# Another order of the first MLP product's seven parts

## The chip, the cores and the metric

The kernel runs on one core of a Trainium2 chip. The metric is the time of one execution on the device in microseconds. The kernel before took 2326.77 us (median of three runs, 2323.07 to 2330.35).

## What is computed

One decoder layer over 2048 tokens of width 1024, all in float32: a norm, an input projection, four token mixers, a group norm, an output projection with a residual, and then the part that matters here, a squared-ReLU MLP of inner width 4096 with a residual and a final norm.

```
h = rms_norm(x, norm2_g)                         # 2048 x 1024
x = x + square(relu(h @ w_mlp_in)) @ w_mlp_out   # 1024x4096, 4096x1024
return rms_norm(x, final_g)
```

## The kernel before, in words

Every float32 product is made of three matmuls in a rounded format. `split` (lines 53 to 58) writes the high part of an operand with a cast on ScalarE (line 54) and the remainder with a subtraction on VectorE (line 58); a product is then high times high, high times low and low times high.

The MLP (class `MLP`) works on halves of 1024 tokens, the second half of the sequence first. Within a half the inner width is cut into two chunks (`c`), and for each chunk there is a first product (tokens times `w_mlp_in`, called IN here) and a second one (hidden times `w_mlp_out`, OUT). So the MLP has eight stages: IN, OUT, IN, OUT for one half and the same for the other. Each stage is a product of two matrices of 2 x 2 blocks, and it is done with seven block products in place of eight, in the manner of Strassen. The tables `FIRST` (for IN) and `SECOND` (for OUT) give for each of the seven the weight blocks, the token or hidden blocks and the blocks of the result: an entry `((a), (b), sign)` is block a plus or minus block b, and with `None` for b it is block a alone. In `FIRST` a token block (k, t) is the half k of the model width and the 512 tokens t of the half; a weight block is (half of the chunk's inner width, half of the model width).

A product has 8 steps (`p`), and a step of an IN stage is 12 matmuls into one PSUM bank of the pool `ps_i`, which has three. What a step needs and leaves:

- the weight side, made two steps ahead (`AHEAD`): one or two loads of 256 KB on SP's queue (lines 1492 and 1508); for a pair of blocks POOL adds or subtracts them (`united`, line 1485); then the cast and the subtraction of `split`;
- the token side, made once for a product, while the product before runs (`tokens_side`, called from `run` at steps 1 to 5): four times one or two loads of `hT` (line 1492), for a pair an addition on POOL (line 1485), and the split into `bh` and `bl`. There are two buffers of each;
- the result: `product_in` takes the PSUM bank to one or two of the four hidden blocks `c`. The first product in the order that reaches a block copies it with ScalarE (line 1563), later ones add to it with VectorE (`gather`, lines 1573 and 1575), and after the last one ScalarE does relu and square in place (lines 1568 and 1569).

`run` works out from the order which product is the first and the last for each block (`ends`). By the place in the order, not by the product, it loads the residual rows `acc` (fourth place, chunk 0) and gets the norm and the transposes of the other half out of `prep` (places one to seven of the first half's second IN stage). OUT stages have their own order, `OUT_ORDER`. Their hidden side (`hidden_side`, line 1544) adds two hidden blocks on POOL for five of the seven products; its result is the tile `s`. `weight_sums` writes sums of `w_mlp_out` blocks to memory during the first half's OUT stages, so that the later stages load them as one block.

Ahead of the MLP stand the mixers and the output projection. While the last rows of the projection run, `prep` normalises the first half's tokens in groups of 256 and stores their transpose `hT` (lines 1460 to 1479) in memory: sixteen tiles, by 512 tokens and 256 columns of the width.

Inside the MLP the order of instructions on each engine is not written out. The program lists the steps, and a planner that simulates the engines gives each instruction a place: an instruction whose operands are there by the simulation can go ahead of earlier ones that still wait. On the chip each engine then runs its list strictly in this order, and waits on semaphores.

Of the kernel before, what the change touches and what calls it, by code (L numbers as in the profile page):

```python
# [1393 lines left out]
}  # L1394
IN_ORDER = (1, 4, 5, 7, 3, 2, 6)
OUT_ORDER = (3, 5, 6, 1, 2, 4, 7)
AHEAD = 2

# [25 lines left out]
class MLP:  # L1424
# [172 lines left out]
    def run(self):  # L1597
# [9 lines left out]
        ends = {}  # L1607
        for order, table, n in ((IN_ORDER, FIRST, 0), (OUT_ORDER, SECOND, 1)):
            seen, last = {}, {}
            for i in order:  # L1610
                for blk, _ in table[i][2]:
# [3 lines left out]
        steps = [(half, c, out, i, p) for half in self.halves for c in range(self.NC) for out in range(2)  # L1615
                 for i in (OUT_ORDER if out else IN_ORDER) for p in range(NP)]
        made, sides = {}, {}
# [25 lines left out]
        for n, (half, c, out, i, p) in enumerate(steps):  # L1643
            if c == 0 and not out and i == IN_ORDER[3]:
                self.acc[p] = accp.tile([128, self.D], F32, tag=f"acc{p}", name="acc")
                with behind(self.tc, SP):
                    nc.sync.dma_start(out=self.acc[p], in_=self.x1[half * self.HT // 128 + p])
            if c == 1 and not out:

                if i == IN_ORDER[0] and p == 0:  # L1650
                    k = self.halves.index(half) + 1
                    more = self.prep(self.halves[k]) if k < len(self.halves) else iter(())
                if n % 4:
                    next(more, None)
                if i == IN_ORDER[-1]:
                    for _ in more:
# [187 lines left out]
```

## Time and profile before

| what | value |
|---|---|
| median of the runs | 2326.77 us |
| the profiled execution: time, span | 2332.89 us, 2331.2 us |
| PE busy | 2156.8 us (93%) |
| VectorE (DVE) busy | 1775.0 us (76%) |
| ScalarE (ACT) busy | 1166.4 us (50%) |
| GpSimd (POOL) busy | 952.8 us (41%) |
| mean granted clock of PE, share of full speed | 0.971 |
| the MLP: first matmul to last | 989.34 to 2312.81 us |

The profile is of one execution. Times in the rows are microseconds from the start of the span, unless ns is said. PE is the matmul engine, PEld its weight loads, SP the engine that issues most loads. A wait is named by the instruction that released it, as `<-ACT bh L54`. L1485 is line 1485 of the kernel. A row of the table by windows gives the window, its length, the busy time of PE, PEld, DVE, ACT and POOL with their instructions (x), PE's mean granted clock as a share of full speed, the busy share of the DMA engines and GB/s.

### The profile page before, as it was taken

The numbers are of one execution on the slowest core, as the hardware profiler recorded it, in microseconds if no ns is written. First come the engines' busy times: TensorE is split into PE (matmuls) and PEld (weight loads), VectorE is DVE, ScalarE is ACT, GpSimd is POOL, SyncE is SP. The second block draws the span as 40 slices with busy tenths as digits, with TensorE's granted clock in tenths as the row PEclk, the third lists the DMA queues.
The fourth block names the chain that finished last, engine by engine and source line by source line (L and its number), as shares of the span: only waits on it lengthen the run. The fifth ranks groups of instructions, "written<-read, shape, count | busy, mean of one in ns | idle before, by whom it ended". The sixth has DMA issues, their size and how long they took to land.

```text
span 2331.2 us, 32435 instructions
## 1 busy us (share of the span) xinstructions
PE 2156.8 (93%) x10077; PEld 1758.3 (75%) x10077; DVE 1775.0 (76%) x3826; ACT 1166.4 (50%) x2349; POOL 952.8 (41%) x988
## 2 busy tenths in 40 slices
PE   5999998997999998799998999898989999999996
PEld 4777777776887887578777777787878787888885
DVE  5887757765676775378899868888878798578797
ACT  4423544444666664257633356543557643567443
POOL 2144343231001011154877633657244665246352
PEclk9999999998999999999999999999999999999998
DMA  7533135237666746999989688979699634578223
GB/s 183 164 83 95 62 96 169 89 131 226 194 173 167 196 139 203 246 260 320 279 239 224 206 252 255 268 211 221 183 281 289 212 114 122 164 224 243 96 82 113
DMA packets 398236, 435.53 MB, mean 187 GB/s; under 512 B 37552, under 2 KB 280272, under 8 KB 397808
## 3 DMA queue, kind: packets, MB, share of 16 engines
q1 hardware_dynamic: 370224, 362.08, 52.1%
q0 software_dynamic: 23232, 65.09, 11.5%
q10 hardware_dynamic: 4608, 6.29, 0.7%
q8 instruction: 80, 1.31, 0.2%
q14 instruction: 92, 0.75, 0.1%
HBM read 370.35 MB, written 96.57 MB: 200 GB/s over the span
## 4 chain that ended last, share of the span: by engine, by line
PE 48%; DVE 9%; DMA 9%; issue 6%; POOL 4%; ACT 3%; SPq 1%; POOLq 0%; DVEq 0%; ACTq 0%
PE po L1583 6%; PE po L1584 6%; PE po L1582 6%; PE pi L1557 5%; PE pi L1559 5%; PE pi L1558 5%; POOL raw L1485 3%; DMA raw<-in_w_mlp_in_dram 3%; DVE wl L58 2%; PE s L1080 2%; PE t L50 2%; PE po L1356 2%; PE po L1358 2%; PE po L1357 2%; DMA raw<-hT 1%
## 5 line engine op out<-in xcount | busy, mean ns | idle before, releaser
L1485 POOL TENSOR_TENSOR raw<-raw 128x512 f32<-128x512 f32 x304 | 447.4, 1485 | 359.8 <-DMA raw<-in_w_mlp_in_dram 188.5
L58 DVE TENSOR_TENSOR wl<-raw,wh 128x512 fp32r<-128x512 f32 x448 | 423.7, 952 | 63.4 <-ACT wh L54 54.6
L1557 PE MATMUL pi<-bh,wh 128*128 128x512 f32 x896 | 357.5, 399 | 36.5 <-ACT c L1563 12.0
L1583 PE MATMUL po<-wl,sh 128*128 128x512 f32 x896 | 352.8, 394 | 22.2 <-DVE wl L58 22.2
L1558 PE MATMUL pi<-bl,wh 128*128 128x512 f32 x896 | 353.6, 395 | 5.8 <-DVE bl L58 5.8
L1559 PE MATMUL pi<-bh,wl 128*128 128x512 f32 x896 | 353.8, 395 | 5.1 <-DVE wl L58 5.1
L1582 PE MATMUL po<-wh,sh 128*128 128x512 f32 x896 | 351.3, 392 | 2.1 <-ACT wh L54 2.1
L1584 PE MATMUL po<-wh,sl 128*128 128x512 f32 x896 | 351.9, 393 | 0.0
L1544 POOL TENSOR_TENSOR s<-c 128x512 f32<-128x512 f32 x160 | 256.1, 1611 | 234.3 <-DVE sl L58 201.8
L54 ACT CAST wh<-raw 128x512 fp32r<-128x512 f32 x448 | 274.5, 615 | 120.0 <-POOL raw L1485 51.4
L58 DVE TENSOR_TENSOR sl<-s,sh 128x512 fp32r<-128x512 f32 x160 | 207.9, 1307 | 35.4 <-ACT sh L54 35.1
L1557 PEld LDWEIGHTS pi<-bh,wh 128*128 128x128 f32 x896 | 170.8, 191 | 80.8 <-ACT c L1563 15.8
L54 ACT CAST sh<-s 128x512 fp32r<-128x512 f32 x160 | 99.4, 621 | 258.7 <-PE po L1583 184.5
L1583 PEld LDWEIGHTS po<-wl,sh 128*128 128x128 f32 x896 | 170.0, 190 | 61.8 <-DVE wl L58 26.3
L1559 PEld LDWEIGHTS pi<-bh,wl 128*128 128x128 f32 x896 | 171.0, 191 | 44.4 <-DVE wl L58 8.1
L1558 PEld LDWEIGHTS pi<-bl,wh 128*128 128x128 f32 x896 | 170.9, 191 | 41.2 <-DVE bl L58 6.3
L1582 PEld LDWEIGHTS po<-wh,sh 128*128 128x128 f32 x896 | 170.0, 190 | 38.0 <-ACT wh L54 2.5
L1584 PEld LDWEIGHTS po<-wh,sl 128*128 128x128 f32 x896 | 169.9, 190 | 35.7 <-DVE sl L58 0.4
L428 PE MATMUL z<-wh,hl 128*128 128x512 f32 (+1 forms) x384 | 150.8, 393 | 18.2 <-ACT hl L54 11.9
L58 DVE TENSOR_TENSOR bl<-raw,bh 128x512 fp32r<-128x512 f32 x112 | 125.4, 1133 | 38.2 <-ACT bh L54 35.6
L429 PE MATMUL z<-wl,hl 128*128 128x512 f32 (+1 forms) x384 | 142.5, 371 | 1.0 <-DVE wl L380 1.0
L430 PE MATMUL z<-wh,hl 128*128 128x512 f32 (+1 forms) x384 | 142.5, 371 | 0.9 <-DVE hl L58 0.9
(361 smaller groups left out, 4222.4 us busy)
## 6 DMA issues: line engine op xcount, KB each, us to landing
raw<-in_w_mlp_in_dram SPq DMA_DIRECT2D x384, 256.0 KB, 4.7
raw<-hT SPq DMA_DIRECT2D x192, 256.0 KB, 4.3
raw<-in_w_mlp_out_dram SPq DMA_DIRECT2D x192, 256.0 KB, 4.3
raw<-s SPq DMA_DIRECT2D x96, 256.0 KB, 2.7
x<-in_x_dram SPq DMA_DIRECT2D x32, 512.0 KB, 6.4
s<-in_w_mlp_out_dram SPq DMA_DIRECT2D x32, 512.0 KB, 6.7
s<-in_w_mlp_out_dram POOLq DMA_DIRECT2D x32, 512.0 KB, 8.0
x<-x POOLq DMA_DIRECT2D x31, 512.0 KB, 5.4
```

What stands on the lines that cost most here:

```text
L54: nc.scalar.copy(out=hi, in_=src)
L58: nc.vector.tensor_tensor(out=lo, in0=src, in1=hi.bitcast(F32), op=SUB)
L428: nc.tensor.matmul(pz, lhsT=hi[:, k, sl], rhs=wh, start=(k == 0), stop=False)
L429: nc.tensor.matmul(pz, lhsT=hi[:, k, sl], rhs=wl, start=False, stop=False)
L1485: self.nc.gpsimd.tensor_tensor(out=raw[:, 0], in0=raw[:, 0], in1=raw[:, 1], op=ADD if sign > 0 else SUB)
L1544: self.nc.gpsimd.tensor_tensor(out=s, in0=src, in1=self.C[b[1], b[0], p], op=ADD if sign > 0 else SUB)
L1557: nc.tensor.matmul(pt, lhsT=wh[:, sl], rhs=bh[:, k], start=(k == 0), stop=False)
L1558: nc.tensor.matmul(pt, lhsT=wh[:, sl], rhs=bl[:, k], start=False, stop=False)
L1559: nc.tensor.matmul(pt, lhsT=wl[:, sl], rhs=bh[:, k], start=False, stop=(k == 3))
L1582: nc.tensor.matmul(po[t], lhsT=sh[:, ts], rhs=vh, start=(p == 0), stop=False)
L1583: nc.tensor.matmul(po[t], lhsT=sh[:, ts], rhs=vl, start=False, stop=False)
L1584: nc.tensor.matmul(po[t], lhsT=sl[:, ts], rhs=vh, start=False, stop=(p == self.NP - 1))
```

## The change

One line: the order in which the seven parts of every IN stage are done. All loops, tables and buffers stay; what follows from the order (which product copies a block first, which one does relu and square, what is loaded ahead of what) follows it.

```
-IN_ORDER = (1, 4, 5, 7, 3, 2, 6)
+IN_ORDER = (2, 4, 1, 5, 7, 3, 6)
```

By `FIRST`, products 2 and 4 use token blocks of the first 512 tokens only, 3 and 5 of the second 512 only, and 1, 6 and 7 of both. Weights are pairs in 1, 2, 5, 6 and 7; token sides are pairs in 1, 3, 4, 6 and 7. The hidden blocks by product, with the number of the product that copies (first) and the one that ends with relu and square (last):

| hidden block | products | first, last before | first, last after |
|---|---|---|---|
| c(0,0) | 1, 4, 5, 7 | 1, 7 | 4, 7 |
| c(0,1) | 3, 5 | 5, 3 | 5, 3 |
| c(1,0) | 2, 4 | 4, 2 | 2, 4 |
| c(1,1) | 1, 2, 3, 6 | 1, 6 | 2, 6 |

## Rows read from the trace of the kernel before

**Rows 1.** The page: engine, busy us (share of the span), instructions.
```profile
PE 2156.8 (93%) x10077; PEld 1758.3 (75%) x10077; DVE 1775.0 (76%) x3826; ACT 1166.4 (50%) x2349; POOL 952.8 (41%) x988
```

**Rows 2.** Busy time by windows: the four IN stages, the last OUT stage.
```profile
989.34:1154.04 164.70, 155.93 (x673) 127.15 (x674) 133.21 (x157) 107.04 (x187) 103.09 (x71) 0.97 0.95 285
...
1324.39:1516.18 191.79, 171.80 (x738) 136.54 (x737) 154.06 (x229) 111.84 (x197) 91.08 (x65) 0.96 0.84 251
...
1678.17:1846.36 168.19, 157.26 (x674) 127.54 (x673) 139.28 (x208) 108.26 (x190) 94.90 (x70) 0.98 0.95 277
...
2005.69:2160.49 154.80, 153.60 (x674) 125.89 (x673) 115.51 (x149) 101.52 (x176) 80.11 (x56) 1.00 0.76 221
2160.33:2312.81 152.48, 152.48 (x673) 125.94 (x671) 129.14 (x204) 65.28 (x116) 65.23 (x43) 1.00 0.27 91
```

**Rows 3.** Busy time by windows, one part each: IN1, IN2, IN3, IN4.
```profile
989.34:1019.99 30.65, 24.47 (x97) 19.12 (x97) 23.64 (x18) 17.28 (x32) 19.94 (x14) 0.84 0.84 247
...
1063.51:1085.27 21.76, 21.76 (x98) 18.02 (x96) 18.23 (x24) 16.86 (x30) 10.01 (x8) 1.00 0.95 311
...
1107.03:1130.96 23.93, 22.21 (x97) 17.86 (x96) 21.27 (x27) 15.12 (x26) 20.21 (x14) 1.00 0.83 229
1130.96:1153.88 22.92, 22.05 (x97) 17.94 (x96) 19.55 (x24) 16.70 (x30) 19.37 (x14) 1.00 0.95 308
...
1461.69:1494.25 32.56, 25.17 (x106) 20.34 (x104) 26.60 (x30) 16.41 (x28) 22.25 (x17) 0.90 0.91 250
...
1799.11:1823.06 23.95, 22.25 (x97) 17.86 (x96) 21.28 (x27) 15.16 (x26) 19.41 (x13) 1.00 0.81 230
1823.06:1846.19 23.13, 22.02 (x97) 17.94 (x96) 21.42 (x24) 17.16 (x32) 19.42 (x13) 1.00 0.89 277
...
2115.35:2138.57 23.22, 22.26 (x98) 17.86 (x97) 20.56 (x27) 15.15 (x26) 19.14 (x13) 1.00 0.86 237
```

**Rows 4.** Timeline of PE, 980 to 1000: the instructions that it waited before.
```profile
989.34 0.80 PE L1557 MATMUL pi<-bh,wh 128*128 128x512 f32 x1 [7.04 <-ACT bh L54]
995.93 0.79 PE L1558 MATMUL pi<-bl,wh 128*128 128x512 f32 x1 [5.80 <-DVE bl L58]
```

**Rows 5.** The chain that ended last, 940 to 1000: start, us, what.
```profile
980.11 2.25 DMA hT<-ht
982.42 4.62 DMA raw<-hT
987.11 1.53 POOL raw L1485
988.67 0.63 ACT bh L54
```

**Rows 6.** Timelines of SP, POOL and DVE at the start of IN1.
```profile
946.74 1.11 SPq L1492 DMA_DIRECT2D raw<-hT  x2
...
984.88 1.26 POOL L1485 TENSOR_TENSOR raw<-raw 128x512 f32<-128x512 f32 x1 [14.06 <-DMA raw<-in_w_mlp_in_dram]
...
989.18 6.14 POOL L1485 TENSOR_TENSOR raw<-raw 128x512 f32<-128x512 f32 x5
...
989.32 8.37 DVE L58 TENSOR_TENSOR bl<-raw,bh 128x512 fp32r<-128x512 f32 x4 [1.80 <-ACT bh L54]
```

**Rows 7.** Timelines of POOL, DVE and PE in IN4's sixth part, product 2.
```profile
2122.11 1.55 POOL L1544 TENSOR_TENSOR s<-c 128x512 f32<-128x512 f32 x1 [2.55 <-ACT c L1569]
...
2121.82 0.68 DVE L58 TENSOR_TENSOR bl<-raw,bh 128x512 fp32r<-128x512 f32 x1
...
2129.67 1.77 DVE L58 TENSOR_TENSOR bl<-raw,bh 128x512 fp32r<-128x512 f32 x1
...
2132.79 0.47 PE L1557 MATMUL pi<-bh,wh 128*128 128x512 f32 x1 [0.96 <-ACT c L1568]
```

**Rows 8.** Windows, IN4's second part; and the lines view of the MLP, relu.
```profile
2027.45:2049.21 21.76, 21.76 (x97) 18.02 (x96) 12.39 (x19) 11.98 (x21) 6.67 (x6) 1.00 0.79 219
...
L1568 ACT ACTIVATE c<-c 128x512 f32<-128x512 f32 x128 | 80.8, 631 | 48.1 <-DVE c L1573 47.7
```

## The prediction

> **What bounds the kernel now.** I read the page's busy shares first: PE is busy 93% of the 2331.2 us span, so only the time in which it waits or runs slowly can be won [rows 1]. Then I cut the trace at the ends of the MLP's eight stages (four first products, "IN", four second ones, "OUT") and read the table by windows. Each stage issues 672 matmuls. The last OUT stage takes 152.5 us with PE busy throughout; the IN stages take 164.7, 191.8, 168.2 and 154.8 us [rows 2]. So the four IN stages lose about 12, 39, 16 and 2 us against a stage that is never held up, and only these stages are reordered.
>
> Cutting once more at the ends of the seven parts shows where. A part that is never held up takes 21.76 us (IN1's fourth part). IN1's first part takes 30.65. The sixth part, product 2, is late in all four stages: 23.93, 32.56, 23.95 and 23.22 us. The seventh, product 6, takes 22.92 in IN1 and 23.13 in IN3. All of these stand in [rows 3].
>
> Two waits explain these. At the start, PE sits idle 7.04 us before the first matmul, at 989.34, and 5.80 us before the second [rows 4]. The chain of waits backwards from there: the norm's last hT store is issued at 980.11 and takes 2.25 us, the load of hT behind it 4.62, POOL's addition 1.53, ScalarE's cast 0.63 [rows 5]. Product 1 adds block (0,0) to block (1,1), which belongs to the second 512 tokens, so its token side waits for the last stores of the norm. In the sixth part POOL has, in its one order, an s addition for OUT's second product ahead of the additions for products 2 and 6; it waits 2.55 us for the square of c(1,0), which product 2 is just finishing, and four steps later PE waits 0.96 us at a step's first matmul [rows 7].
>
> **The change part by part.** Nothing is added or removed: the same 56 steps a stage, 40 weight additions (products 1, 2, 5, 6, 7), 20 token additions (1, 3, 4, 6, 7), gathers and copies. Products 5, 7, 3 keep their sequence and 4 stays second; 2 comes from the sixth place to the first and 1 from the first to the third. Counting POOL's additions by part (a part's own 8 for weights and the 4 for the next part's tokens) the old stage has 12, 0, 12, 12, 0, 12, 12, the new one 12, 4, 8, 12, 12, 4, 8.
>
> *Start of IN1.* Product 2 needs block (0,0) alone: four loads, no addition, and hT tiles stored by the norm's first two groups. Such loads (the first operands of product 1's sums) were issued from 946.74 on in the trace of before, while the projection still ran [rows 6]. The chain of rows 5 then no longer ends at the first matmul. What is late next is the first weight: its addition ran from 984.88 for 1.26 us [rows 6], and with a cast of 0.63 PE can start at 986.77, 2.57 us sooner if the weight comes no earlier, and up to 7.04 if it does. The 5.80 us went to bl: four subtractions took 8.37 us while POOL ran five additions in 6.14 [rows 6]; three of the five were product 1's token additions, which are gone here. The first part lost 30.65 - 21.76 = 8.89 us, of which 5.80 is that gap and the rest PE at a mean granted clock of 0.84 after the two gaps (1.2 GHz for part of it) [rows 3]. Gain between 2.6 (the gap stays, made by product 4's token additions) and 7.04 + 8.89 = 15.9. I take 2.57 + 8.89 = 11, nearest to the weight's own row.
>
> *Fifth to seventh part.* The sixth becomes product 3, behind product 7 as before; the seventh, product 6, has 8 additions instead of 12, since the next stage's first token side is a single. What parts six and seven lose now: 2.17 + 1.16, 10.80 + 0, 2.19 + 1.37, 1.46 + 0 = 19.2 us [rows 3]. Part of it moves. The s addition needs c(0,0) and c(1,0); c(1,0) is final in part two now, c(0,0) in product 7, the new fifth part, which has 12 additions. The wait for a square then stands there. In the old order the sixth part lost 2.2, 2.2 and 1.5 us in IN1, IN3 and IN4; I keep 1.5 in each of the four stages, 6. In IN2 the other half's norm is done beside the IN stage's parts, and of the 10.80 us I keep half, 5.4, since its end falls about there in both orders. So the body gains 19.2 - 6 - 5.4 = 7.8, between 0 (all of it moves) and 19.2.
>
> *Product 4.* It now does c(1,0)'s last gather, so 16 relu and square operations come on top of ScalarE's 11.98 us in that part (IN4) [rows 8]: 11.98 + 16 x 0.63 = 22.1 us in a part of 21.76. Product 1 behind it has no copies and no relu, so ScalarE catches up there, with three PSUM buffers between it and PE. I take 0.5 us a stage, 2; the bounds are 0 and the third rival's 20.
>
> *The rest.* Product 1 in the third part gathers twice on DVE with 8 additions on POOL instead of product 5's one gather with 12: lighter, 0. IN2's first part and the OUT stages are loaded as before. The acc loads go by place in the order, not by product, and stay in the fourth part, on SP's queue behind loads of a pair product, as before. The planner orders every engine anew, so stalls that hang on where a cast was queued can come or go: 0, with the widest single stall of the body, 10.8 us, as the bound on either side.
>
> Sum: 11 + 7.8 - 2 = 17 us. Against the profiled execution's 2332.89 us (span 2331.2, 1.7 us around it) that is 2316; that execution lies 6.1 above the median of the runs, 2326.77, so 2310 for the median.
>
> A subtraction alone took 0.68 us, the next one beside POOL 1.77 [rows 7]; a lone addition took 1.26 [rows 6]. A part with 12 additions and 12 subtractions, if no two overlap, needs 12 x 1.26 + 12 x 0.68 = 23.3 us, over 21.76; one with 8 needs 18.2. The Trainium skill, page SBUF — State Buffer, section SBUF: two separate sides, says that GpSimd and a VectorE operation with two SBUF inputs take a shared port in turn, one fully blocking the other; the rows agree. By that rule the turn time of a stage (60 additions, 84 subtractions, the same in both orders) can't shrink, only be spread; that speaks against the body's gain and is the first rival.
>
> **Rivals.** *First: the contention only moves* (faster, by the start alone). All of POOL's additions and DVE's subtractions stay, and the new parts four and five have 12 each with the s additions behind them; what parts six and seven won is lost there. For it: the s addition's wait follows c(0,0) by its place in the code. Against: product 7 behind product 5 was part four before, with the same 12 additions, and took 21.76 us in IN1 [rows 3]. 11 us gained: 2316.
>
> *Second: no change.* The first weight gates the start (2.6 us won), product 4's token additions come into the same burst and hold bl again, and the body stands as in the first rival: 2324. For it: that burst's later additions are there in either order. Against: the token side would be cast before the burst.
>
> *Third: slower.* ScalarE in product 4. Each relu waits for its gather on DVE: over all stages 47.7 us in 128 relus, 0.37 each [rows 8]. In product 4 a step's casts and copy don't fill that time if the planner puts relu ahead of them, and the wait is then up to a whole gather, taken as a lone DVE operation of 0.68 [rows 7]: 22.1 + 8 x 0.68 = 27.5 us, 5.8 over the part's 21.76, four times 23, less some 3 that product 1 gives back: 20 us. With 11 gained at the start, 2326.8 + 9 = 2336. For it: no other part holds 36 ScalarE operations. Against: three PSUM buffers take up two steps' delay, and at 0.37 a relu the excess is 3.3 us a part, within that. It decides from about 0.55 us a relu.
>
> **Chances and range.** Forecast 0.45, first rival 0.22, second 0.16, third 0.13, anything else 0.04. A measurement of this kernel tells about 0.3%, 7 us, from no change: 2320 to 2334. Faster is the forecast, nearly all of the first rival: 0.66; same 0.19; slower 0.15. The likeliest case alone spans 2294 to 2319. The range goes from 2285 (start 15.9, body 19.2, and 7 of the 10.8 left to the planner) to 2336, the third rival.
>
> **What would show it.** First matmul of the MLP within about 5 us of the last matmul of the output projection, no gap of over 2 us before the second, and a first part of IN1 under 24 us: the start's step. Sixth and seventh part at 21.8 in IN1, IN3, IN4: the body's. An s addition in the fifth part that waits for a square, and a part of over 23 us there: the first rival. ScalarE's idle in product 4 near zero with PE waiting for copies there: the third. The prediction is wrong in its main step if PE still waits over 10 us between the projection and the second matmul.

## The result and the profile after

The changed kernel takes 2348.44 us, the median of 4 runs (2342.93 to 2350.93), the kernel before 2328.42 beside it: ratio 1.0086, 95% interval 1.0067 to 1.0104. It is slower by 0.86%, some 20 us. The forecast was 2310, faster, and the time lies outside its range. The profiled execution took 2350.93 us with a span of 2349.2.

The page's busy shares hardly move [rows 1]. The same instructions run; of the 18.0 us by which the span is longer, PE is busy for 10.8 more and idle for 7.2 more.

```profile
PE 2167.6 (92%) x10077; PEld 1761.2 (75%) x10077; DVE 1769.7 (75%) x3826; ACT 1162.1 (49%) x2349; POOL 950.9 (40%) x988
```

The stages of the changed kernel by windows, IN1 to IN4 and OUT4 (answers to [rows 2]): length, then busy time of PE, PEld, DVE, ACT, POOL, PE's granted clock, DMA share, GB/s.

```profile
985.97:1154.14 168.17, 158.22 (x673) 127.75 (x672) 122.47 (x152) 102.45 (x180) 92.16 (x65) 0.98 0.89 271
1329.20:1525.95 196.75, 173.90 (x737) 136.92 (x736) 152.66 (x229) 111.92 (x199) 92.08 (x66) 0.96 0.82 248
1687.50:1860.90 173.40, 160.54 (x673) 128.16 (x672) 138.03 (x208) 106.84 (x189) 95.29 (x71) 0.97 0.93 269
2020.50:2178.40 157.90, 154.99 (x673) 127.01 (x672) 121.93 (x149) 100.51 (x176) 88.06 (x60) 0.99 0.77 224
2178.40:2330.91 152.51, 152.51 (x673) 125.94 (x671) 129.17 (x204) 65.31 (x116) 65.07 (x43) 1.00 0.28 91
```

All four IN stages are longer, by 3.5, 5.0, 5.2 and 3.1 us; OUT4 is not. The parts (answers to [rows 3]): IN1's first, fifth and sixth, the fifth of IN2 and of IN3, then IN4's second (product 4) and fifth.

```profile
985.97:1012.77 26.80, 23.64 (x97) 19.09 (x96) 13.05 (x13) 12.71 (x25) 19.07 (x14) 0.94 0.90 286
1078.58:1110.62 32.04, 25.43 (x98) 18.64 (x96) 28.07 (x28) 19.61 (x34) 26.73 (x17) 0.95 0.72 215
1110.62:1132.41 21.79, 21.79 (x98) 18.02 (x97) 17.80 (x27) 16.70 (x29) 8.72 (x6) 1.00 1.04 309
1448.69:1481.47 32.78, 25.95 (x106) 19.52 (x105) 30.45 (x40) 18.33 (x33) 23.06 (x15) 0.95 0.67 208
1786.69:1817.45 30.76, 25.61 (x97) 18.46 (x96) 27.34 (x27) 18.54 (x32) 26.78 (x17) 0.94 0.73 217
2042.29:2064.05 21.76, 21.76 (x98) 18.02 (x97) 13.30 (x19) 18.74 (x35) 4.71 (x3) 1.00 0.68 189
2107.57:2134.90 27.33, 24.42 (x97) 18.88 (x96) 26.11 (x24) 17.80 (x31) 24.77 (x16) 0.94 0.73 219
```

The fifth part, product 7, is where the time went: 32.04, 32.78, 30.76 and 27.33 us against 21.76 for a part never held up, 35.9 us over in the four stages. In the old order the same product, then the fourth part, was 10.7 us over, of which 8.8 in IN2. POOL did 15 to 17 operations in the part where it did 8 to 10 before. The rest cancels out: the old sixth part, product 2's, was 16.6 over and is gone, product 6's 2.5 are gone; product 1 in the third part is 6.3 over (5.5 of it in IN2), product 5 7.4 worse (5.9 in IN2), the OUT stages 4.0, and 1.6 lies in small differences.

Of the 9.0 us by which IN3's fifth part is over, PE is idle for 5.2, all of it waiting for weights (waits view of that part: who waited for whom, us in total, times, the longest):

```profile
PE pi L1559 <- DVE wl L58: 2.7, 5, 0.9
PE pi L1557 <- ACT wh L54: 2.4, 2, 1.5
```

For the rest PE is busy longer, 25.61 us for 21.76. Part of that is the clock: behind waits of 1.51 and 0.85 us the granted clock is 0.5 (1.2 GHz) from 1810.20 to 1813.61, and nine matmuls from 1809.96 on take 3.75 us, where nine of a clean part take 2.04. IN1's part shows the same; in IN2 and IN4 PE waits mostly for gathers on DVE, 5.6 and 2.9 us.

The timeline of POOL through that part in IN3, changed kernel (start, us, what, in brackets the idle time before it and its releaser):

```profile
1789.17 1.29 POOL L1485 TENSOR_TENSOR raw<-raw 128x512 f32<-128x512 f32 x1 [0.42 <-DMA raw<-in_w_mlp_in_dram]
1790.94 2.99 POOL L1485 TENSOR_TENSOR raw<-raw 128x512 f32<-128x512 f32 x2 [0.48 <-DMA raw<-in_w_mlp_in_dram]
1794.10 1.53 POOL L1485 TENSOR_TENSOR raw<-raw 128x512 f32<-128x512 f32 x1 [0.18 <-DMA raw<-in_w_mlp_in_dram]
1795.58 1.76 POOL L1544 TENSOR_TENSOR s<-c 128x512 f32<-128x512 f32 x1
1797.30 1.75 POOL L1485 TENSOR_TENSOR raw<-raw 128x512 f32<-128x512 f32 x1
1799.01 1.74 POOL L1544 TENSOR_TENSOR s<-c 128x512 f32<-128x512 f32 x1
1800.71 2.96 POOL L1485 TENSOR_TENSOR raw<-raw 128x512 f32<-128x512 f32 x2
1804.37 1.62 POOL L1544 TENSOR_TENSOR s<-c 128x512 f32<-128x512 f32 x1 [0.69 <-ACT c L1569]
1805.95 10.17 POOL L1485 TENSOR_TENSOR raw<-raw 128x512 f32<-128x512 f32 x6
```

And the kernel before in product 7's part of IN3, where it waits again and again, mostly for its loads:

```profile
1758.11 2.60 POOL L1485 TENSOR_TENSOR raw<-raw 128x512 f32<-128x512 f32 x2 [1.78 <-DMA raw<-in_w_mlp_in_dram]
1762.57 3.00 POOL L1485 TENSOR_TENSOR raw<-raw 128x512 f32<-128x512 f32 x2 [1.85 <-DMA raw<-in_w_mlp_in_dram]
1766.97 3.00 POOL L1485 TENSOR_TENSOR raw<-raw 128x512 f32<-128x512 f32 x2 [1.40 <-DVE bl L58]
```

A POOL that waits for loads keeps up. In the changed kernel it has a backlog from 1790.94 to 1816.12, with 0.87 us of idle time in all, and an operation takes up to 1.76 us, 1.60 on the mean of the part, where a lone one takes 1.29 (mean before, in product 7's part: 1.39). DVE, beside it, takes up to 1.78 us for a subtraction, 1.31 on the mean (before 0.92). A gather, which has one operand in PSUM, stays at 0.68, and so does the subtraction at 1804.15, which starts in POOL's pause of 0.69 us:

```profile
1797.81 1.78 DVE L58 TENSOR_TENSOR wl<-raw,wh 128x512 fp32r<-128x512 f32 x1
1801.22 0.68 DVE L1573 TENSOR_TENSOR c<-pi,c 128x512 f32<-128x512 f32 x1
1803.13 1.10 DVE L58 TENSOR_TENSOR wl<-raw,wh 128x512 fp32r<-128x512 f32 x1 [1.23 <-ACT wh L54]
1804.15 0.68 DVE L58 TENSOR_TENSOR sl<-c,sh 128x512 fp32r<-128x512 f32 x1
```

The Trainium skill, page SBUF — State Buffer, section SBUF: two separate sides, has this split: a VectorE operation with two SBUF inputs and a GpSimd operation that reads SBUF shut each other out for a whole instruction. The trace agrees, with 0.68 us in POOL's pause and 1.10 to 1.78 in the other subtractions shown. At the start of IN1 before, one subtraction was shut out for longer than an instruction: 6.56 of the 8.37 us in [rows 6] are its own, beside all five additions.

At the start PE no longer waits before the first matmul. It waits earlier, in the tail of the projection (changed kernel, timelines of ACT, PE, POOL and DVE, and the first matmul):

```profile
957.88 0.62 ACT L54 CAST bh<-raw 128x512 fp32r<-128x512 f32 x1 [4.83 <-DMA raw<-hT]
958.82 0.80 PE L1356 MATMUL po<-h,hi 128*128 128x512 f32 x1 [5.48 <-ACT hi L54]
975.72 1.28 POOL L1485 TENSOR_TENSOR raw<-raw 128x512 f32<-128x512 f32 x1 [3.93 <-DMA raw<-in_w_mlp_in_dram]
977.03 0.62 ACT L54 CAST wh<-raw 128x512 fp32r<-128x512 f32 x1 [5.92 <-POOL raw L1485]
977.69 1.43 DVE L58 TENSOR_TENSOR wl<-raw,wh 128x512 fp32r<-128x512 f32 x1 [5.85 <-ACT wh L54]
979.04 0.68 DVE L1477 TENSOR_TENSOR ht<-tp,g 128x512 f32<-128x512 f32 x1
979.77 0.66 PE L50 MATMUL tp<-ident,h 128*128 128x128 f32 x4 [2.64 <-DVE ht L1477]
985.97 0.39 PE L1557 MATMUL pi<-bh,wh 128*128 128x512 f32 x1
995.79 0.62 ACT L54 CAST bh<-raw 128x512 fp32r<-128x512 f32 x1 [3.93 <-POOL raw L1485]
997.45 0.50 PE L1557 MATMUL pi<-bh,wh 128*128 128x512 f32 x1 [3.16 <-ACT c L1563]
```

Work that the new order makes early stands ahead of the tail's own. On ScalarE's list a cast of product 2's tokens waits 4.83 us for its load, the projection's cast `hi` stands right behind it, and PE waits 5.48 us (6.0 to 7.0 in four more programs with the changed order). The subtraction of product 2's weight stands on DVE's list ahead of the norm's copy of a transpose, and waits 5.85 us for a cast that waits for a load; the transposes wait behind it, and PE 2.64 us. How much of this is a loss shows only from a common point. I took the 200th projection matmul before the last one, and from there the times in ten of the programs run here, five with each order (the records let this be placed to about 1 us):

```
                                      projection's    first MLP      end of the
                                      last matmul     matmul         first part
before                                66.9 us         74.3           105.0
old order, all five                   66.9 to 69.5    74.0 to 76.2   101.2 to 105.7
after                                 78.5            78.7           105.5
changed order, all five               76.9 to 78.6    77.4 to 78.9   104.5 to 107.3
```

The gap is closed from the wrong side: the projection ends some 10 us later. From the common point to there PE's waits add up to some 15 us where they were 8.4 (13.6 to 15.5 in the five, 7.9 to 9.5 in the old five), and its mean granted clock is 0.91 where it was 0.97 (0.89 to 0.91, 0.95 to 0.97). The end of the first part, 105.0 and 105.5, has not moved. The profiled execution of before had also come to that common point late, at 915.0 us, where the other nine stood at 905 to 910. Counted from that point the two profiled executions are some 26 us apart, the medians of the runs 20: single executions scatter by a few us, and the figures below, of one execution each, with them.

### The profile page after: what moved, and what is told of

The parts are those of the page before. It is cut to its first block, busy times and chain, and to the rows that moved or that the text cites. A ratio compares the mean times of both kernels' runs of the same rounds, so it can differ in the third digit from the quotient of the medians.

```text
span 2349.2 us, 32424 instructions
## 1 busy us (share of the span) xinstructions
PE 2167.6 (92%) x10077; PEld 1761.2 (75%) x10077; DVE 1769.7 (75%) x3826; ACT 1162.1 (49%) x2349; POOL 950.9 (40%) x988
## 3 DMA queue, kind: packets, MB, share of 16 engines
q8 instruction: 80, 1.31, 0.2%
## 4 chain that ended last, share of the span: by engine, by line
PE 34%; DVE 8%; DMA 7%; issue 4%; POOL 3%; ACT 2%; SPq 1%; POOLq 0%; DVEq 0%; ACTq 0%
PE po L1583 6%; PE po L1582 6%; PE po L1584 6%; PE pi L1557 5%; PE pi L1559 5%; PE pi L1558 5%; DMA raw<-in_w_mlp_in_dram 4%; DVE wl L58 3%; DMA raw<-hT 2%; DVE sl L58 2%; POOL raw L1485 2%; DVE acc L1573 1%; POOL s L1544 1%; SPq L1492 1%; DVE bl L58 1%
## 5 line engine op out<-in xcount | busy, mean ns | idle before, releaser
L1557 PE MATMUL pi<-bh,wh 128*128 128x512 f32 x896 | 360.0, 402 | 34.7 <-ACT c L1563 15.5
L1583 PEld LDWEIGHTS po<-wl,sh 128*128 128x128 f32 x896 | 170.0, 190 | 66.0 <-DVE wl L58 30.5
L58 DVE TENSOR_TENSOR bl<-raw,bh 128x512 fp32r<-128x512 f32 x112 | 108.1, 978 | 51.9 <-ACT bh L54 50.4
L1573 DVE TENSOR_TENSOR c<-pi,c 128x512 f32<-128x512 f32 x160 | 109.4, 684 | 45.2 <-PE pi L1559 32.7
```

Of the source, the lines that this page charges most:

```text
L58: nc.vector.tensor_tensor(out=lo, in0=src, in1=hi.bitcast(F32), op=SUB)
L1557: nc.tensor.matmul(pt, lhsT=wh[:, sl], rhs=bh[:, k], start=(k == 0), stop=False)
L1583: nc.tensor.matmul(po[t], lhsT=sh[:, ts], rhs=vl, start=False, stop=False)
```

## The experiments

I compare from the end of IN1's first part to the MLP's last matmul ("body"), which leaves the start's scatter out, and by product 7's part in the four IN stages. It was 1292.8 before and 1318.1 after: 25.3 us, as much as product 7's part lost, 25.2. Each ratio is to runs of the kernel before taken beside that kernel; their medians lie between 2326.77 and 2332.04, so ratios compare better than medians.

```
                               median   ratio to before [95%]     body     product 7's part, IN1 to IN4
before                         2328.42  1                         1292.8   21.8  30.5  22.8  22.6
after                          2348.44  1.0086 [1.0067, 1.0104]   1318.1   32.0  32.8  30.8  27.3
after, s additions held        2346.05  1.0071 [1.0050, 1.0092]   1314.6   29.8  32.8  30.4  24.5
after, casts held              2343.39  1.0070 [1.0051, 1.0089]   1310.5   27.5  31.1  27.8  22.1
after, both held               2334.82  1.0011 [0.9996, 1.0026]   1299.2   23.7  31.3  23.9  21.8
s held, 6's tokens late        2346.86  1.0074 [1.0051, 1.0096]   1314.8   25.9  30.9  26.0  22.6
order 2, 1, 4, 5, 7, 3, 6      2345.81  1.0066 [1.0043, 1.0088]   1314.3   28.5  33.6  27.2  26.1
order 4, 1, 5, 7, 3, 2, 6      2326.43  0.9986 [0.9969, 1.0003]   1291.7   22.2  30.2  23.3  22.1
before, 4 additions more       2339.47  1.0057 [1.0043, 1.0070]   1309.9   23.5  33.1  27.2  26.2
before, 8 additions more       2358.19  1.0144 [1.0128, 1.0160]   1325.4   28.1  38.5  28.5  29.9
before, s additions held       2321.13  0.9959 [0.9945, 0.9973]   1282.2   22.8  29.5  22.0  21.9
before, held outside OUT1      2317.30  0.9951 [0.9929, 0.9972]   1284.9   21.9  30.5  21.9  21.9
4, 1, 5, 7, 3, 2, 6, so held   2317.02  0.9941 [0.9921, 0.9961]   1284.8   21.8  31.9  23.0  21.8
so held, casts held too        2319.73  0.9964 [0.9949, 0.9980]   1285.7   22.4  31.8  22.5  21.8
```

"Held" means that an instruction is kept behind the last one that the program had listed on its engine, so that the planner can't pull it ahead into product 7's part.

*The additions for OUT's second product held* (first theory: these three s additions, moved into the fifth part, make it late):

```
+            with behind(self.tc, POOL) if i == OUT_ORDER[1] else ExitStack():
                 self.nc.gpsimd.tensor_tensor(out=s, in0=src, in1=self.C[b[1], b[0], p], ...)
```

> The changed order, with one thing added: the s additions of OUT's second product are queued behind all of POOL's additions of the IN stage, so none of them runs in IN. Theory A (pile-up): in the changed order c(0,0) and c(1,0) are both final with product 7, so three s additions join its 12 additions and its subtractions; without them the fifth part falls from 32.2, 32.9, 30.9 and 27.5 us to 22 to 25 in IN1, IN3 and IN4, and the time from 2348 to 2320-2330. Theory B (no light part): product 1 with 8 additions stands where product 4 with none stood ahead of 5 and 7, and POOL gets no lead; the fifth part stays at 27 to 32 us and the time within 5 us of 2348.

(The expectation counts a part to the end of its last matmul, 0.16 us more than the table.) Missed: the fifth part gave back 2 us in IN1 and 0.3 in IN3, although POOL's operations there fell from 17 to 14, and the total is the rival's, which the orders below test. DVE still did 27, each about 1.0 us:

```profile
1785.37:1815.81 30.44, 25.70 (x97) 19.28 (x96) 26.99 (x27) 19.52 (x35) 21.73 (x14) 0.89 0.79 232
```

*The direct casts for OUT's first product held as well* (these need c(0,0) alone, which product 7 finishes):

```
+        with behind(self.tc, ACT) if i == OUT_ORDER[0] else ExitStack():
             split(self.nc, sh, sl, src)
```

> As the run with the s additions held back, and the casts and subtractions of c(0,0) for OUT's first product (sh, sl), of which four ran in the fifth part, held back to the end of the IN stage too. Theory A: they are the rest of the pile-up; the fifth part comes to 21.8-22.5 us and the time is equal to that run's or up to 5 us lower. Theory B: no more than 3 us from 2348. If holding them back starves the first steps of OUT, OUT's first part grows over 23 us and shows it.

Now the part is nearly clear, 23.7 and 23.9, with the same 14 operations on POOL and five fewer on DVE, and the total fell by 11 us, further than the 0 to 5 expected (IN3's fifth part by windows, and POOL's timeline there):

```profile
1777.35:1801.26 23.91, 22.70 (x98) 17.62 (x96) 20.69 (x22) 16.30 (x28) 21.95 (x14) 1.00 0.92 279
```
```profile
1781.60 20.05 POOL L1485 TENSOR_TENSOR raw<-raw 128x512 f32<-128x512 f32 x12 [0.44 <-DMA raw<-in_w_mlp_in_dram]
```

POOL alone, 12 additions in 20.05 us without a pause, still fits a part.

*The casts held alone:* the second edit without the first.

> The changed order with only the casts and subtractions of the four hidden tiles that OUT's first product takes without an addition held in their program place (the additions are not held). It takes 4 of 16 subtractions out of part five and leaves 17 additions: 29.6 us in turn against 32.3. Theory (the sum of the part decides): part five falls by 2 to 4 us to 27 to 30 in IN1 and IN3, and the total by 4 to 10 us, to 2338 to 2345. Rival (these subtractions and casts themselves block the queues of ScalarE and VectorE ahead of the weights; that is why holding both kinds cleared the part): part five falls to 22 to 25 and the total to 2332 to 2337.

Within the theory's ranges: 27.5 and 27.8, total 2343.39. Neither kind alone clears the part in IN1 and IN3, both together nearly do. IN2's, 30.5 before, stays at 31 to 33 with any of the three holds.

```profile
1785.12:1812.88 27.76, 23.52 (x98) 17.52 (x96) 20.68 (x22) 16.47 (x28) 25.22 (x17) 1.00 0.83 240
```

*Other orders.* The rival theory was that product 7 suffers from what stands ahead of it: the new order has no light product before it. First an order with product 1 ahead of 5 and 7, but products 3, 2, 6 behind:

```
+IN_ORDER = (4, 1, 5, 7, 3, 2, 6)
```

> Order (4, 1, 5, 7, 3, 2, 6): 4 and 1 of the old order change places, 2 stays sixth. c(1,0) is final only in the sixth part, as before, but product 1 with 8 additions stands ahead of 5 and 7, as in the changed order. Theory A: product 7 (fourth part) takes 22 to 23 us as before, the sixth part is late as before, and the time is 2318 to 2330 (the start gains 3 to 8). Theory B: product 7 takes 27 to 32 us in each stage and the time is 2340 to 2350.

Then the reverse, product 4 directly ahead of 5 and 7, and 3, 6 behind:

```
+IN_ORDER = (2, 1, 4, 5, 7, 3, 6)
```

> Order 2, 1, 4, 5, 7, 3, 6: the changed order with products 4 and 1 exchanged, so that product 4 (without paired token blocks) stands ahead of 5 and 7, as in the order before. What follows product 7 (3 and 6, and OUT's first products) is as in the changed order. Theory (pile-up from what follows: product 6's token additions and OUT's additions run beside product 7): part five stays at 28 to 32 in IN1 and IN3, and the total within 6 us of the changed order, 2342 to 2354. Rival (what stands ahead of product 7 decides: a product with few additions lets GpSimd get ahead): part five falls to 22 to 24 in IN1 and IN3 and the total to 2322 to 2332.

The first ran clean (23.33 in IN3, 9 operations on POOL), the second late (27.18, a little under the 28 expected, with 17). What follows product 7 decides, not what stands ahead: with 2 behind 3, POOL has no token additions to do after product 7's list, and the s additions wait for c(1,0) until product 2; with 6 there it has four token additions, and the s additions come too.

```profile
1741.56:1764.89 23.33, 22.62 (x98) 17.79 (x97) 18.22 (x24) 16.86 (x30) 12.06 (x9) 1.00 0.97 314
```
```profile
1784.48:1811.66 27.18, 22.77 (x97) 17.62 (x96) 25.41 (x25) 16.36 (x29) 25.84 (x17) 1.00 0.74 226
```

*Product 6's token loads issued later,* behind product 3's weight loads, on top of the held additions:

```
+            with behind(self.tc, SP) if i == 6 else ExitStack():
                 raw = self.load(...)
...
+            p0 = 3 if i == IN_ORDER[5] else 1
+            if not out and p == p0:
                 part = side(nxt)
...
+            if not out and p0 <= p < p0 + 5:
                 next(part, None)
```

> The changed order, with the additions of OUT's second product held in their program place (as in new_s) and the token loads of product 6 issued in the queue behind weight loads of product 3 and two steps later, so that product 6's four token-pair additions run in part six (product 3) instead of at the end of part five (product 7). Theory (the part's sum of GpSimd additions at 1.26 us and VectorE subtractions at 0.68 us decides, because the two ran in turn where they were thick): part five of IN1 and IN3 falls from 29.8 and 30.4 to about 22 to 24 (10 additions and 16 subtractions, 23.5 us), IN4's to 21.8; part six, with 4 more additions and none of its own, stays under 23; the total falls by 12 to 20 us against the run with the first edit alone (2346.05), to about 2326 to 2334. Rival (the part is late because of what the two products before it left behind, not because of what runs in it): part five stays at 29 to 31 and the total at 2343 to 2350.

Half a hit and no gain: the total is the rival's. The fifth part fell by 4 us with POOL at 11, which the rival denied, but not to 22 to 24, and the sixth rose to 23.0, 24.7 and 24.9 (IN3's fifth and IN4's sixth part by windows; then POOL and ACT in the latter):

```profile
1790.93:1816.91 25.98, 23.36 (x98) 17.42 (x96) 23.91 (x28) 18.25 (x33) 17.18 (x11) 1.00 0.64 186
2132.60:2157.50 24.90, 22.55 (x97) 17.79 (x96) 20.90 (x29) 17.89 (x32) 15.13 (x10) 1.00 1.05 303
```
```profile
2138.23 1.29 POOL L1485 TENSOR_TENSOR raw<-raw 128x512 f32<-128x512 f32 x1 [2.30 <-DMA raw<-hT]
```
```profile
2139.55 0.62 ACT L54 CAST bh<-raw 128x512 fp32r<-128x512 f32 x1 [2.43 <-POOL raw L1485]
```

The load comes too late now, and ScalarE's cast waits for it. The subtraction behind the cast stands on DVE's list ahead of product 3's gathers, and PE waits 1.31 us for one of these at 2142.24. Here the late load cost as much as the early addition.

*Additions that nobody waits for,* put into the order before, where product 7's part was clean: one more behind each of product 7's eight weight additions in a stage, then behind every second (`if i == 7 and p % 2`). They write the spent half of the load's buffer.

```
+        x = self.united(raw, sign)
+        if i == 7:
+            self.nc.gpsimd.tensor_tensor(out=raw[:, 1], in0=raw[:, 0], in1=raw[:, 1], op=ADD)
+        return self.parts(x)
```

> The order before, in which product 7's part (the fourth) ran clean, with one more GpSimd addition of 128x512 behind each of product 7's eight weight additions; it overwrites the second block of the pair, which nobody reads any more, so no value changes and nobody waits for it but the buffer's next load. It brings the part from 9 additions to 17, the changed order's count in its late fifth part. Theory (the number of GpSimd additions beside the part's VectorE work makes it late, whatever they compute): the fourth part goes from 21.8, 22.8 and 22.6 to 28 to 33 in IN1 and IN3 and 24 to 28 in IN4, VectorE's mean operation there from some 0.7 to 0.9 us or more, and the total rises by 15 to 35 us, to 2345 to 2365. Rival (the part is late because of who waits for whom: the hidden-side additions and the next token block stand ahead of weights in the queue): additions that nobody waits for cost under 2 us a part and under 8 us in all.

> The same with four more additions instead of eight (every second weight tile of product 7): 13 additions and 16 subtractions in the part, 27.3 us if they went in turn. Theory: the fourth part takes 24 to 28 us in IN1 and IN3 and 22 to 24 in IN4, and the total rises by 6 to 18 us. Rival (who waits for whom): under 1 us a part and under 5 us in all.

Total +31.4 and +12.7 us for 32 and 16 additions: 1.0 and 0.8 us each, though no value hangs on them and only the buffer's next load has to wait for them. IN3's product 7 by windows, four more and eight more (the windows hold 11 and 14, the rest ran ahead of them):

```profile
1751.11:1778.27 27.16, 24.16 (x97) 18.74 (x96) 19.81 (x24) 18.16 (x32) 16.59 (x11) 0.94 0.86 273
```
```profile
1760.76:1789.29 28.53, 24.56 (x98) 18.84 (x97) 21.23 (x25) 16.71 (x30) 21.93 (x14) 0.94 0.77 245
```

The totals and most parts lie where expected; IN1 with four more (23.5) is under, IN4 with both (26.2, 29.9) over, and DVE's mean of 0.85 in IN3 with eight (21.23 / 25) stays short of the 0.9 expected. The pile alone makes the part late: with eight more, POOL's list runs without a gap (L1533 is the added one), and PE waits in IN3's part for weights and for gathers alike, 1.9 and 2.0 us.

```profile
1763.56 2.99 POOL L1485 TENSOR_TENSOR raw<-raw 128x512 f32<-128x512 f32 x2
1766.63 1.64 POOL L1533 TENSOR_TENSOR raw<-raw 128x512 f32<-128x512 f32 x1
```

*The order before with the additions held,* everywhere and then everywhere but in OUT1 (a flag `late` that is false for the first half's first stage):

```
+            with behind(self.tc, POOL) if late and i == OUT_ORDER[1] else ExitStack():
```

> The order before, with the s additions of OUT's second product held back behind the additions of the IN stage. Theory A: the sixth part (product 2), 23.9, 32.6, 24.0 and 23.2 us before, comes to 21.8-22.5 in IN1, IN3, IN4 and to 24-32 in IN2; the time is 2312 to 2322. Theory B, by which these additions matter little: 2325 to 2331.

> The order before, with the additions of OUT's second product held in their program place in every stage but the first OUT stage, where holding them lengthened the stage by 10 us. Theory (the additions are the cause of the late sixth part, and in the first OUT stage alone they are needed early): IN2's sixth part stays at about 23.8 (32.6 before), those of IN1, IN3, IN4 at 21.8 (IN1's back to 23.9, as its additions are not held), OUT1 comes back to 170 to 172, and the time is 2306 to 2316, below the 2321.13 with all of them held. Rival (OUT1's length is a matter of where the weight sums fall and goes its own way): OUT1 stays at 178 to 181 and the time at 2318 to 2324.

The stall of rows 7 goes: the sixth part is 21.8 in IN1, IN3 and IN4 and 23.8 in IN2, where it was 32.6 (by windows, everywhere held, IN3 and IN2):

```profile
1789.46:1811.22 21.76, 21.76 (x98) 18.02 (x96) 20.98 (x28) 16.36 (x28) 16.75 (x11) 1.00 1.02 283
1460.07:1483.82 23.75, 23.02 (x106) 18.72 (x104) 20.79 (x28) 15.31 (x26) 15.15 (x12) 1.00 1.04 294
```

OUT1 grew to 180.6 from 170.5 with all held and came back to 171.9 in the second kernel, but IN2 then took 186.4 instead of 179.1. The bodies are 1282.2 and 1284.9: what OUT1 is spared IN2 pays, and the second theory's 2306 to 2316 is missed by 1 us.

*Order 4, 1, 5, 7, 3, 2, 6 with the additions held outside OUT1,* and with the casts held too:

> Order 4, 1, 5, 7, 3, 2, 6 with the same additions held outside the first OUT stage. Theory: IN2's sixth part falls from 32.1 to about 24, IN3's and IN4's from 23.6 to 21.8, OUT1 stays at about 172; against the same order without the edit (2326.43) a gain of 8 to 14 us, 2312 to 2319. Rival (the late part only moves on): the gain is under 4 us, 2322 to 2328.

> Order 4, 1, 5, 7, 3, 2, 6 with the additions of OUT's second product and the direct casts of OUT's first product both held in their program place in all stages but the first OUT stage. Theory (the sums of IN2 and of the parts that took these tiles early): IN2's sixth part stays at about 24, IN2's fourth (31.9) and IN3's (23.0) fall by up to 2 us, and the time is 2306 to 2316, under the 2317.02 without the casts. Rival (with the additions gone no part of this order is over its sum but IN2's, which has other causes): the time is 2314 to 2320, not to be told from the run without the casts.

The first is a hit but for OUT1, which took 175.0 where 172 was expected: 2317.02, against before 0.9941 where the same order without the hold had 0.9986, some 10 us. It beats both kernels, before by 0.59% (0.39% to 0.79%). The casts add nothing there, 2319.73, as the rival had it.

## Why the prediction was wrong

*Start of IN1, forecast -11.* From the common point it measured 0.5 the other way. That the first matmul would follow the projection closely, with no gap before the second, came true, and so the sign that was to show this step wrong, over 10 us of waiting between the two, did not come; the step failed all the same. It took the projection's end as fixed. It did not count what the earlier loads, casts and subtractions, moved ahead of the tail's own work on ScalarE's and VectorE's lists, would do to that tail. And the first part was to lose nothing in place of 8.89 us; it lost 5.04. The 3.16 us wait at 997.45 is ScalarE's copy behind a cast that waited 3.93 for a token addition, near to the second rival, in which these additions hold the subtractions for `bl`. The five programs of the old order lose 5.5 to 8.9 us there, the five of the changed one 4.6 to 7.7, so the scatter alone is nearly half of the term.

*Fifth to seventh part, forecast -7.8.* This is the step that failed most. These parts were 20.2 us over before and are 36.9 over now: +16.6. That parts six and seven would be clean is right (IN2's sixth is 1.0 over), and so is the s addition that waits for a square in the fifth (0.69 us at 1804.37). The term mis-sized is "I keep 1.5 in each of the four stages" (and 5.4 more in IN2): the fifth part measured 10.3, 11.0, 9.0 and 5.6. The price was taken from the sixth part of before, for one wait. What is paid in the new fifth part is a full list. The count of 12 POOL operations there was made by the program's steps. The trace has 17: PE runs two steps behind POOL, product 3 has no weight additions, so product 6's four token additions follow product 7's at once, and three s additions come on top; beside them DVE has product 7's weights, product 3's tokens and four direct subtractions for OUT, 16 by the program. In turn, as the prediction's own paragraph on the shared port has it, 17 x 1.26 + 16 x 0.68 = 32.3 us; IN1 measured 32.0, IN3 30.8. The paragraph was weighed with 12 and 12, 23.3 us.

That sum gives the size, not the last 3 us, and its counts are of two kinds: the windows of IN1 and IN3 hold 19 and 18 subtractions, some of them for later weights, which would make 34.3 and 33.7. With 16 and 12 as the program has them: with the additions held 28.5 against 29.8 and 30.4, with the casts held 29.6 against 27.5 and 27.8, with both 25.8 against 23.7 and 23.9; before, with 9 and 16, 22.2 against 21.8 and 22.8. IN4 has 16 and 16, 31.0 by the sum, and measured 27.3. One thing that the sum leaves out stands in the rows: PE's mean granted clock in IN3's part was 0.89 with the additions held, where the part took longer than the sum, and 1.00 with the casts or both held, where it took less.

*Product 4, forecast +2.* It cost nothing in IN1, IN3 and IN4: 21.76 us with ScalarE at 18.74, where the step had 22.1; IN2's is 1.0 longer. The relus waited longer for their gathers, 54.2 us in all against 47.7 [rows 8], 0.42 each, below the 0.55 from which the third rival decides. In the lines view of the changed kernel, its operations and what they waited for:

```profile
L1568 ACT ACTIVATE c<-c x128: 623/632/636, 1017.4 to 2179.3; 128x512 f32<-128x512 f32 x128
...
  DVE c L1573: 54.2, 80
```

The right sign came from none of the cases: the only one on the slow side put its price on ScalarE.

*The rest, forecast 0.* The body's 25.3 us are 16.6 from parts five to seven, 4.7 from parts one to four of the stages (without IN1's first) and 4.0 from the OUT stages, where OUT1 alone was 4.5 longer. No run isolates these last two: in OUT1 the weight sums and in IN2 the next half's norm run beside the products. OUT1 takes 174.9 to 176.8 in every run of the changed order or of 2, 1, 4, 5, 7, 3, 6, and 170.5 to 173.9 in before and in the runs of it whose s additions were not held there; but order 4, 1, 5, 7, 3, 2, 6 took 171.9, 175.0 with the additions held and 172.2 with the casts too. The cause stays open. The prediction's list of late parts also left out the longest of IN2 and IN3, their first, 33.79 and 32.82 us before and 35.17 and 32.18 after; in IN3 PE waits 6.4 and 6.5 us there for ScalarE's copies. In order 4, 1, 5, 7, 3, 2, 6 they take 23.68 and 21.76, but other parts and OUT stages take most of that back; no run isolates why.

*First rival, "the contention only moves".* Its mechanism is the one that the runs bear out, but its price was capped at what parts six and seven had won. Gathered in one part, the contention cost more here than it had spread over three.

## What to carry to other kernels

Before a reordering, count each engine's list by the stretch in which it runs, run-ahead included, and not by the step that issues it; a stretch with no work of its own for an engine is a gap into which the next block's work falls. When a gap at a seam is to be closed, time both sides from a point ahead of the seam, in more than one execution. Work that can be pulled early isn't free early: keep it behind the work that the present part needs. And look for the largest loss before choosing what to reorder.

## What the runs showed of the hardware

A GpSimd addition of 128x512 costs time even if nobody waits for its result: 32 of them cost 31.4 us of the total, 16 cost 12.7, where they fell beside VectorE's subtractions. Where both lists were full (IN3's fifth part, changed kernel) the additions took 1.60 us on the mean, up to 1.76, where a lone one took 1.29, and the subtractions 1.31, up to 1.78, where a lone one took 0.68, while gathers out of PSUM stayed at 0.68. One subtraction was held for 6.56 us beside five additions in a row (start of IN1 before). And in the part where POOL did 12 additions in a row in 20.05 us PE was only 2.1 us late with 22 operations on VectorE; with 27 there, and as many on POOL, it was 8.7 late, at a mean granted clock of 0.89 where it had been 1.00.
